# Eight lasting rooms for the expert weights, and the one-hot products of pair 14 moved ahead of pair 15's down projection

## The chip, the cores and the metric

The kernel runs on one core of a Trainium2 chip. TensorE (PE) multiplies, VectorE (DVE), ScalarE (ACT) and GpSimd (POOL) do the rest, and SP only issues transfers. SP, ACT and POOL each feed a queue of the same 16 DMA engines: in the profile q1 is SP's queue, q10 ACT's, q0 POOL's. The metric is the device time of one execution in microseconds (us), lower is better.

## The reference

Three transformer blocks follow one another on 512 tokens of width 1024, all in f32. The first holds windowed attention with a gated convolution, and then the mixture of experts that the change touches. The other two (attention and a squared-ReLU feed-forward each) come after it and are not touched. Cut to what matters, the mixture of experts is:

```python
h2 = rmsnorm(x, norm2_g)
g_logits = h2 @ w_rg + b_rg                # 4 groups
grp = argmax(g_logits)
e_in = (h2 @ w_re + b_re)[..., grp, :]     # the 8 experts of the group
top_p, top_i = top_k(softmax(e_in), 2)     # 2 experts for each token
gates = p_grp * top_p / sum(top_p)
...
hid = silu(xb @ w_gate[e]) * (xb @ w_up[e])     # 1024 -> 256, 32 experts
y   = hid @ w_down[e]                           # 256 -> 1024
x   = x + sum over a token's two experts of gate * y
```

The weights of the 32 experts are 100.7 MB, and every one is read once.

## The kernel before

**Pairs and pieces.** The experts are worked on two at a time: pairs 0 to 15, a pair on the two halves of TensorE. The weights of a pair come as three pieces of 2.10 MB, 128 partitions x 4096 f32: the two halves of gate and up (here gu p.0 and gu p.1) and the down projection (dn p). `moe_order` (L1605) gives the order of use: gu 0.0, gu 0.1, gu 1.0, gu 1.1, dn 0, gu 2.0, gu 2.1, dn 1 and so on to dn 14, dn 15. Places in this order are counted from 0.

**Rooms and rings.** A piece needs a room in SBUF. `c.rings` lists kinds of rooms, each with a function that makes the tiles, the number of rooms, and how many are taken: ring 0 the `raw` tiles that all other weights use (three of 1.05 MB), 1 two tiles `ew`, 2 the two slabs `esH`, `esL`, 3 the tile `ey` (tag `y0`), 4 four tiles `t`, and before the change 5 the tiles `we` (tags `wh` and `wl`, once each) and 6 the tiles `eq` (tag `yq`, once). A piece can lie in one room, or as two halves in rooms of two rings. `moe_jobs` (L1581) writes down for each piece which rings it takes; `Core._dma` (L89) issues the pieces strictly in the order of that list and stops at the first whose ring is not made yet or has no room; `_free` (L107) gives a room back when TensorE's use of the piece has been written into the program, and calls `_dma` again. In SP's queue the transfer itself then waits for the TensorE instructions that read the room last. A room of four 128x512 tiles is filled by four transfers with rows of 2 KB, a tile of 128x1024 by one with rows of 4 KB; the rows of the larger tiles are moved in pieces of 8 KB.

**Ahead of the routing.** While the attention's output projection still runs, five pieces are loaded (places 0, 4, 5, 6, 7 of the order). `moe` (L2015) then makes rings 3 and 6 and calls `_dma`: place 2 goes out in four transfers (`eq`). Place 1 is next in the list and takes ring 5, which is made only after `m.gates()`; so it, place 3 (ring 3) and place 8 are issued there, by ACT (`c._dma(queue=nc.scalar)`).

**The routing.** `Moe.norm` and `Moe.route` turn the tokens into rows and write them to DRAM: eight transfers of 0.26 MB with rows of 512 B (`hrows`, L1691, on ACT's queue), four of them in `route`. DVE works out the slots, and POOL gathers the token rows of a pair from `hrows` (`gather`, L1854) into `xg`; the gather waits for all eight writes. `turn` (L1894) turns them, and `gu` of pair 0 begins.

**The loop over pairs.** In turn p TensorE does gu of pair p, and then, for pair o = p - 1, the down projection. Up to pair 11 POOL scatters the result to DRAM (`yrows`, L1861). After the scatter of pair 11 `results` (L1870) reads them back, two of four blocks first (tiles `yr` and `y`, 512 rows of 2 or 4 KB altogether per block pair), and `add_results` turns and adds them. The last four pairs are added by one-hot products instead (`comb`, L1958): for each of eight blocks d of X, matmuls of y (two parts) with a one-hot matrix C, and an addition by DVE (L1960).

Before the change the products of pairs 12 and 13, four matmuls a block, are spread over turns 15 and 16; those of pairs 14 and 15, four a block, are done together in the last loop ("lastcomb"), between the first matmuls of the next block of the network:

```python
    for d in range(NB + 2):
        if d < NB:
            comb(NP - 2, d)
        if 1 <= d <= NB:
            nn[3](d - 1, X[:, d - 1])
```

Of the kernel before, what the change touches and what calls it, by code (L numbers as in the profile page):

```python
# [8 lines left out]
F32 = mybir.dt.float32  # L9
F32R = mybir.dt.float32r  # L10
# [7 lines left out]
D = 1024  # L18
NB = 8
EPS = 1e-6  # L20
NEG = -1e30
NRAW = 3
NSPL = 4
SPL = 512
# [14 lines left out]
class Core:  # L39


    def __init__(self, ctx, tc, aps):
        self.tc, self.nc, self.a = tc, tc.nc, aps
        self.ctx = ctx
        self.const = ctx.enter_context(tc.tile_pool(name="const", bufs=1))
        self.slab = ctx.enter_context(tc.tile_pool(name="slab", bufs=1))
        self.wp = ctx.enter_context(tc.tile_pool(name="wp", bufs=1))
        self.xs = ctx.enter_context(tc.tile_pool(name="xs", bufs=1, side="right"))
        self.wr = ctx.enter_context(tc.tile_pool(name="wr", bufs=1, side="right"))
        self.tmp = ctx.enter_context(tc.tile_pool(name="tmp", bufs=1, side="right"))  # L50
        self.ps = ctx.enter_context(tc.tile_pool(name="ps", bufs=1, space=bass.MemoryType.PSUM))
        self.dram = ctx.enter_context(tc.tile_pool(name="dr", bufs=1, space=bass.MemoryType.DRAM))
        self.jobs = []
        self.groups = []
        self.n_dma = 0
        raw = lambda: self.wr.tile([128, 2048], F32, name="raw", tag="raw", bufs=NRAW)
        self.rings = [[raw, NRAW, 0], None, None, None, None, None, None]
        self.n_split = 0
        self.cur = 0
        self.turns = 0  # L60
        self.now = 0
        self.blk_off = 0
        self.side = []
        self.due = []
        self.ratio = 1.0
        self.raw = {}
        self.spl = {}
        self.lows = []
        self.keep = {}
# [1504 lines left out]
NP = 16  # L1574
# [6 lines left out]
def moe_jobs(c):  # L1581

    gs = {}
    order = moe_order()

    def piece(i, *ring):
        n = order[i]
        w = c.a["e_w"][n // 3]
        o = 2 * (n % 3)
        if len(ring) == 1:  # L1590
            gs[n] = c.add_job(w[o:o + 2].rearrange("e p n -> p e n"), [(4096, 1)], split=False, ring=ring[0])
        else:
            gs[n] = sum((c.add_job(w[o + e], [(2048, 1)], split=False, ring=ring[e]) for e in range(2)), [])

    rooms = [(2,), (3,), (2,), (1,), (1,), (0, 0), (0, 4)]
    piece(0, 2)
    piece(4, 2)
    yield
    for i, ring in ((5, (1,)), (6, (1,)), (7, (0, 0)), (2, (6, 6)), (1, (5, 5)), (3, (3,)), (8, (0, 4))):
        piece(i, *ring)  # L1600
    for i in range(9, len(order)):
        ring = rooms.pop(0)
        if ring == (3,) and i > order.index(3 * NS + 3):
            ring = rooms.pop(0)
        rooms.append(ring)  # L1605
        piece(i, *ring)
    for n in order:
        c.groups += gs[n]
    yield
# [13 lines left out]
class Moe:  # L1623
# [327 lines left out]
    def comb(self, X, d, slots):  # L1951

        c, nc = self.c, self.c.nc
        acc = c.bank("S")
        n = 0
        for Y, C in slots:
            for y in Y:
                nc.tensor.matmul(acc, y[:, d * 128:d * 128 + 128], C, start=n == 0, stop=n == 2 * len(slots) - 1)  # L1958
                n += 1
        nc.vector.tensor_add(X[:, d], acc, X[:, d])  # L1960
# [47 lines left out]

        return self.pool2.tile([128, 4096], F32, name="ey", tag="y0")

    def quarters(self):
        return Row([self.pool2.tile([128, D], F32, name="eq", tag="yq", bufs=4) for _ in range(2)])


def moe(c, X, nn, next_g):  # L2015
    nc = c.nc
    c.mark("moe")
    m = c.moe
    m.pool2 = c.pool(m.es, "moe2")
    c.rings[3] = [m.early, 1, 0]  # L2020
    c.rings[6] = [m.quarters, 2, 0]
    c._dma()
    m.route(X)

    ohs = {}

    def onehot(p, n=2):
        ohs[p] = n, m.onehot(n, m.pos[:, :, 2 * p:2 * p + 2 * n])

    def slots(p):  # L2030
        n, oh = ohs[p]
        m.slots(n, oh, m.idc[:, p:p + n], m.idg[:, p:p + n], p < 2)

    def slots2(p):
        n, oh = ohs.pop(p)
        m.slots2(n, oh, m.info[:, :, p:p + n], m.gate[:, p:p + n], m.rs[:, p:p + n], m.idc[:, p:p + n], m.dest[:, p:p + n])

    gather = lambda p: m.gather(m.idg[:, p:p + 1], p)
    xg = {}
    for p in range(2):  # L2040
        onehot(p, 1)
        slots(p)
        xg[p] = gather(p)
    m.gates()
    c.rings[4] = [lambda: Row([c.t512() for _ in range(4)]), 1, 0]
    turns = iter(("wh", "wl"))

    def halves():
        tag = next(turns)
        return Row([c.wp.tile([128, SPL], F32, name="we", tag=tag, bufs=NSPL) for _ in range(4)])  # L2050

    c.rings[5] = [halves, 2, 0]
    c._dma(queue=nc.scalar)
    xt = {0: m.turn(xg.pop(0))}
    slots2(0)
    slots2(1)
    C = {}
    Y = {}
    held = []

    def w():

        release()
        j, r = c.take_raw()
        held.append(j)
        if len(c.jobs[j][0].shape) == 3:
            return [r[:, :2048], r[:, 2048:]]
        j, r2 = c.take_raw()
        held.append(j)
        return [r, r2]  # L2070

    def release():
        while held:
            c._free(held.pop(0))

    comb = lambda q, d: m.comb(X, d, [(Y[q], C[q]), (Y[q + 1], C[q + 1])])
    c.mark("experts")
    onehot(2)
    ht = {}
    for p in range(NP + 1):  # L2080
        if p < NP:
            hd = m.gu(xt.pop(p), w, m.rs[:, p:p + 1])
            release()
        if p == 0:
            slots(2)
            slots2(2)
        if p + 2 < NP:
            xg[p + 2] = gather(p + 2)
        if p + 1 < NP and p < 1:
            xt[p + 1] = m.turn(xg.pop(p + 1))  # L2090
        o = p - 1
        q = (o // 2 - 1) * 2
        ds = [] if q < NS else list(range(4)) if o % 2 == 0 else list(range(4, 8))
        for d in ds[:2]:
            comb(q, d)
        if o >= 0:
            tile = lambda dt: m.pool2.tile([128, D], dt, name="y", tag="yq", bufs=4)
            if o == NS:
                y = m.pool2.tile([128, 4, D], F32R, name="y4", tag="y0")
            if o < NS:  # L2100
                Y[o] = (tile(F32),)
            elif o < NP - 2:
                Y[o] = (y[:, 2 * (o - NS)], y[:, 2 * (o - NS) + 1])
            else:
                Y[o] = (tile(F32R), tile(F32R))
            m.down(ht.pop(o), w(), m.gate[:, o:o + 1], Y[o])
            release()
            if o < NS:
                m.scatter(o, Y[o][0])
            if o == NS - 1:  # L2110
                rooms = (lambda: Row([c.wp.tile([128, SPL], F32, name="yr", tag="wh", bufs=NSPL) for _ in range(4)]),
                         lambda: Row([tile(F32), tile(F32)]))
                res = [m.results(i, rooms[i]()) for i in range(2)]
            if o >= NP - 2:
                C[o] = m.spread(m.idc[:, o:o + 1], True)
        if 1 <= p < NP - 1:
            xt[p + 1] = m.turn(xg.pop(p + 1))
        for d in ds[2:]:
            comb(q, d)
        if p < NP:  # L2120
            ht[p] = m.turn_hid(hd)
        if o in (NS, NS + 1):
            b = 2 * (o - NS)
            for i in range(2):
                m.add_results(X, b + i, res[i])
            if o == NS:
                res = [m.results(2 + i, rooms[i]()) for i in range(2)]
            else:
                for q in (NS, NS + 1):
                    C[q] = m.spread(m.idc[:, q:q + 1], False)  # L2130
        if 1 <= p < 7:
            slots(2 * p + 2)
            slots2(2 * p + 2)
        if p < 6:
            onehot(2 * p + 4)
    m.beyond(X)
    c.mark("lastcomb")
    nn = c.norm_begin(next_g)
    accs = [c.bank(), c.bank()]
    c._split(c.cur + 1)  # L2140
    c._lows()
    for d in range(NB + 2):
        if d < NB:
            comb(NP - 2, d)
        if 1 <= d <= NB:
            nn[3](d - 1, X[:, d - 1])
            nc.sync.dma_start(c.xdr[:, d - 1], X[:, d - 1])
        if d >= 2:
            for acc in accs:
                for _ in c.block(1, *nn[:2], acc, first=d == 2, last=d == NB + 1, x0=d - 2):  # L2150
                    pass
    m.es.close()
    return nn[:3], accs
# [169 lines left out]
```

## Time and profile before

| | us |
|---|---|
| three runs, median (lowest to highest) | 1871.85 (1870.95 to 1873.17) |
| the profiled execution, its own time | 1871.83 |
| its span, first to last instruction | 1870.0 |
| expert stage: token rows complete, gather issued | 357.3 |
| first expert matmul | 364.9 |
| last loop begins, ends | 627.0, 648 |

All times below are us from the start of the span. The profiled execution agrees with the median; outside the span lie 1.8 us.

### The profile page before, as it was taken

How to read it: one execution, taken by the hardware profiler on the slowest of the kernel's cores; microseconds unless marked ns; L12 is line 12 of the kernel's file. 1: busy time of each engine (PE TensorE's matmuls, PEld its weight loads, DVE VectorE, ACT ScalarE, POOL GpSimd, SP SyncE). 2: the span in 40 equal slices, each digit the busy share in tenths (PEclk: the TensorE clock that was granted, in tenths of full speed). 3: DMA queues.
4: the chain of work that ended last, by engine and by line, in shares of the span. 5: the costliest groups of instructions: out<-in, count | busy, mean ns of one | idle time of the engine just before them, and what ended most of it. 6: DMA issues, size and time to landing. Idle time of an engine off the chain costs nothing.

```text
span 1870.0 us, 23372 instructions
## 1 busy us (share of the span) xinstructions
PE 1777.3 (95%) x8722; PEld 1326.1 (71%) x8722; DVE 1041.5 (56%) x1915; ACT 718.8 (38%) x1418; POOL 359.4 (19%) x392
## 2 busy tenths in 40 slices
PE   8999999799786999999999999999999999999998
PEld 6777787533233686667888888878777788888887
DVE  5765446543113767765655555564776565555555
ACT  6444334211000456664433333333666443333334
POOL 3212012111111251001211111121444221111111
PEclk9999999799997999999999999999999999999999
DMA  6124346599999320202322322243221322222321
GB/s 246 68 65 162 135 156 236 186 399 421 422 422 416 99 94 26 77 29 85 113 90 91 112 90 91 104 127 119 76 60 57 103 100 96 107 90 92 111 91 46
DMA packets 71831, 266.99 MB, mean 143 GB/s; under 512 B 24561, under 2 KB 31089, under 8 KB 46752
## 3 DMA queue, kind: packets, MB, share of 16 engines
q1 hardware_dynamic: 55120, 229.51, 33.2%
q0 software_dynamic: 9936, 27.47, 4.3%
q10 hardware_dynamic: 6656, 8.45, 1.3%
q8 instruction: 72, 1.18, 0.3%
q14 instruction: 47, 0.39, 0.1%
HBM read 251.57 MB, written 18.87 MB: 145 GB/s over the span
## 4 chain that ended last, share of the span: by engine, by line
PE 56%; DVE 6%; ACT 3%; issue 1%; DMA 0%; POOL 0%; POOLq 0%; DVEq 0%; ACTq 0%
PE psacc L227 15%; PE psacc L229 15%; PE psacc L228 15%; PE psT L709 2%; PE psO L861 2%; DVE wl L134 1%; PE psT L341 1%; PE psO L1440 1%; PE psS L1497 1%; PE psS L227 1%; PE psS L1185 1%; ACT wh L125 1%; PE psS L228 1%; PE psS L229 1%; ACT p L696 1%
## 5 line engine op out<-in xcount | busy, mean ns | idle before, releaser
L134 DVE TENSOR_TENSOR wl<-raw,wh 128x512 fp32r<-128x512 f32 x466 | 402.7, 867 | 246.3 <-ACT wh L125 244.8
L227 PE MATMUL psacc<-xh,wh 128*128 128x512 f32 x1008 | 407.4, 404 | 6.6 <-ACT wh L125 6.0
L125 ACT CAST wh<-raw 128x512 fp32r<-128x512 f32 x466 | 285.5, 617 | 321.6 <-PE psacc L228 272.4
L228 PE MATMUL psacc<-xl,wh 128*128 128x512 f32 x1008 | 394.6, 391 | 1.6 <-DVE xl L251 1.6
L229 PE MATMUL psacc<-xh,wl 128*128 128x512 f32 x1008 | 394.7, 392 | 0.1
L227 PEld LDWEIGHTS psacc<-xh,wh 128*128 128x128 f32 x1008 | 190.0, 189 | 56.0 <-issue 14.2
L229 PEld LDWEIGHTS psacc<-xh,wl 128*128 128x128 f32 x1008 | 189.8, 188 | 41.5 <-DVE wl L134 0.6
L228 PEld LDWEIGHTS psacc<-xl,wh 128*128 128x128 f32 x1008 | 190.3, 189 | 35.7 <-DVE xl L251 3.2
L227 PE MATMUL psacc<-uh,wh 128*128 128x512 f32 x480 | 187.0, 390 | 2.6 <-DVE x L453 2.6
L229 PE MATMUL psacc<-uh,wl 128*128 128x512 f32 x480 | 186.8, 389 | 0.0
L228 PE MATMUL psacc<-ul,wh 128*128 128x512 f32 x480 | 186.7, 389 | 0.0
L421 POOL TENSOR_TENSOR t<-t,rstd 128x512 f32<-128x512 f32 x64 | 82.9, 1295 | 526.6 <-ACT t L420 526.6
L453 DVE TENSOR_TENSOR x<-psacc,x 128x512 f32<-128x512 f32 x120 | 82.7, 689 | 125.4 <-PE psacc L229 125.4
L227 PEld LDWEIGHTS psacc<-uh,wh 128*128 128x128 f32 x480 | 90.1, 188 | 22.3 <-issue 3.8
L379 POOL TENSOR_TENSOR ss<-ss,t 128x512 f32<-128x512 f32 (+1 forms) x49 | 58.5, 1193 | 234.9 <-ACT t L372 234.6
L229 PEld LDWEIGHTS psacc<-uh,wl 128*128 128x128 f32 x480 | 90.1, 188 | 18.9
L228 PEld LDWEIGHTS psacc<-ul,wh 128*128 128x128 f32 x480 | 90.1, 188 | 18.5
L243 ACT CAST uh<-t 128x512 fp32r<-128x512 f32 x64 | 39.7, 621 | 131.3 <-DVE t L422 131.3
L709 PE MATMUL psT<-cst,p 128*128 128x128 f32 x448 | 77.1, 277 | 13.4 <-ACT p L696 12.6
L709 PEld LDWEIGHTS psT<-cst,p 128*128 128x128 f32 x448 | 55.2, 140 | 42.6 <-ACT p L696 22.6
L420 ACT ACTIVATE t<-psacc 128x512 f32<-128x512 f32 x64 | 38.3, 599 | 80.8 <-PE psacc L229 80.8
L1914 DVE SCALAR_TENSOR_TENSOR hd<-psS,rs,sl 128x256 f32<-128x256 f32 x16 | 7.7, 484 | 107.9 <-ACT sl L1913 107.9
(493 smaller groups left out, 2707.7 us busy)
## 6 DMA issues: line engine op xcount, KB each, us to landing
raw<-ffn SPq DMA_DIRECT2D x64, 1024.0 KB
ew<-e_w SPq DMA_DIRECT2D x14, 2048.0 KB
raw<-e_w SPq DMA_DIRECT2D x17, 1024.0 KB
esH<-e_w SPq DMA_DIRECT2D x7, 2048.0 KB
esL<-e_w SPq DMA_DIRECT2D x7, 2048.0 KB
ey<-e_w SPq DMA_DIRECT2D x5, 2048.0 KB
raw<-w_in_a SPq DMA_DIRECT2D x8, 1024.0 KB
raw<-od_qk SPq DMA_DIRECT2D x8, 1024.0 KB
```

The source lines that it names most:

```text
L125: nc.scalar.copy(h[:, :n], r)
L134: self.nc.vector.tensor_sub(l, r, h)
L227: nc.tensor.matmul(acc, wh, xh, start=first, stop=False)
L228: nc.tensor.matmul(acc, wh, xl, start=False, stop=False)
L229: nc.tensor.matmul(acc, wl, xh, start=False, stop=last)
L243: nc.scalar.copy(h, src)
L379: self.nc.gpsimd.tensor_add(s, s, q)
L420: nc.scalar.activation(r, acc, AF.Relu)
L421: nc.gpsimd.tensor_mul(r2, r, st["r2"])
L453: nc.vector.tensor_add(X[:, d], acc, X[:, d])
L709: nc.tensor.transpose(t[:, o:o + 128], p[:, m * 128:m * 128 + 128], c.ident)
L861: self.c.nc.tensor.matmul(o[64 * hh:64 * hh + 64], self.V[:, kb, v:v + 64], pt[hh][:, kb], start=kb == 0, stop=kb == 3, skip_group_check=True)
```

## The change

- The one-time rooms are laid out as follows: ring 5 four tiles `wl`, ring 8 a half `yq` (place 1 of the order takes 8 and 5, once); ring 7 four tiles `wh`, ring 6 a half `yw`. Rooms (7, 6) become a lasting room, used in rotation up to place 30 (gu 10.1).
- The rotation has eight rooms and not seven: (2,), (2,), (1,), (1,), (0, 0), (7, 6), (3,), (0, 4). A piece takes the room of the piece eight places before it (seven before the change), the tenth piece that of the first.
- Five pieces are loaded during the output projection as before, now places 0, 2, 3, 4, 5. All rings but 4 are made at the start of `moe`, so places 1, 6, 7 and the first half of 8 go out there on SP: 14 transfers, 7.34 MB, where four transfers of 2.10 MB went out. ACT issues only the second half of place 8 after the gates.
- The results y of pairs 0 to 11 rotate over two tiles `yq` and not four; pair 14 and 15's, and the second room of `results`, take `yq` and `yw`.
- The one-hot products of pairs 12 and 13 are all done in turn 15; those of pair 14 alone, two matmuls for each of eight blocks, in turn 16 ahead of pair 15's down projection; the last loop does pair 15 alone, two matmuls a block.

```diff
-    rooms = [(2,), (3,), (2,), (1,), (1,), (0, 0), (0, 4)]
+    rooms = [(2,), (2,), (1,), (1,), (0, 0), (7, 6), (3,), (0, 4)]
+    last = {(7, 6): order.index(3 * NS - 1), (3,): order.index(3 * NS + 4)}
     piece(0, 2)
-    piece(4, 2)
+    piece(2, 2)
     yield
-    for i, ring in ((5, (1,)), (6, (1,)), (7, (0, 0)), (2, (6, 6)), (1, (5, 5)), (3, (3,)), (8, (0, 4))):
+    for i, ring in ((3, (1,)), (4, (1,)), (5, (0, 0)), (1, (8, 5)), (6, (7, 6)), (7, (3,)), (8, (0, 4))):
         piece(i, *ring)
     for i in range(9, len(order)):
-        ring = rooms.pop(0)
-        if ring == (3,) and i > order.index(3 * NS + 3):
-            ring = rooms.pop(0)
-        rooms.append(ring)
-        piece(i, *ring)
+        while i > last.get(rooms[0], i):
+            rooms.pop(0)
+        rooms.append(rooms.pop(0))
+        piece(i, *rooms[-1])
...
-    def quarters(self):
-        return Row([self.pool2.tile([128, D], F32, name="eq", tag="yq", bufs=4) for _ in range(2)])
+    def half(self, tag):
+
+        return Row([self.pool2.tile([128, D], F32, name="eh", tag=tag, bufs=2) for _ in range(2)])
...
+    quarters = lambda tag: Row([c.wp.tile([128, SPL], F32, name="we", tag=tag, bufs=NSPL) for _ in range(4)])
     c.rings[3] = [m.early, 1, 0]
-    c.rings[6] = [m.quarters, 2, 0]
+    c.rings[5] = [lambda: quarters("wl"), 1, 0]
+    c.rings[6] = [lambda: m.half("yw"), 1, 0]
+    c.rings[7] = [lambda: quarters("wh"), 1, 0]
+    c.rings[8] = [lambda: m.half("yq"), 1, 0]
     c._dma()
     m.route(X)
...
-    c.rings[5] = [halves, 2, 0]
     c._dma(queue=nc.scalar)
...
-    comb = lambda q, d: m.comb(X, d, [(Y[q], C[q]), (Y[q + 1], C[q + 1])])
+    comb = lambda qs, d: m.comb(X, d, [(Y[q], C[q]) for q in qs])
...
-        q = (o // 2 - 1) * 2
-        ds = [] if q < NS else list(range(4)) if o % 2 == 0 else list(range(4, 8))
-        for d in ds[:2]:
-            comb(q, d)
+        qs = {NP - 2: (NS, NS + 1), NP - 1: (NP - 2,)}.get(o)
+        ds = [] if qs is None else list(range(NB))
+        for d in ds[:4 if o == NP - 2 else NB]:
+            comb(qs, d)
...
-        for d in ds[2:]:
-            comb(q, d)
+        for d in ds[4:] if o == NP - 2 else []:
+            comb(qs, d)
...
         if d < NB:
-            comb(NP - 2, d)
+            comb((NP - 1,), d)
```

## Rows read from the trace of the kernel before

**Rows 1.** The page, slices of 46.75 us: DMA share in tenths, and GB/s.

```profile
DMA  6124346599999320202322322243221322222321
GB/s 246 68 65 162 135 156 236 186 399 421 422 422 416 99 94 26 77 29 85 113 90 91 112 90 91 104 127 119 76 60 57 103 100 96 107 90 92 111 91 46
```

**Rows 2.** Windows of the expert stage: length, busy us by engine, PE clock, DMA share, GB/s.

```profile
343.00:352.00 9.00, 7.61 (x40) 5.61 (x38) 5.95 (x26) 3.42 (x6) 0.00 (x0) 0.64 0.77 263
352.00:356.00 4.00, 1.08 (x20) 0.59 (x18) 2.73 (x12) 0.96 (x3) 0.00 (x0) 0.93 0.72 199
356.00:361.00 5.00, 0.27 (x4) 0.18 (x4) 4.00 (x23) 0.20 (x1) 3.04 (x4) 0.50 0.32 93
...
388.00:470.00 82.00, 78.00 (x462) 31.55 (x462) 30.68 (x86) 9.58 (x19) 13.16 (x13) 1.00 1.02 420
470.00:553.00 83.00, 64.94 (x287) 23.29 (x284) 11.72 (x20) 7.30 (x14) 9.11 (x9) 0.94 1.02 421
```

**Rows 3.** Timeline of POOL: start, length, instruction, idle time before it and its releaser.

```profile
357.29 1.10 POOL L1854 DMA_INDIRECT xg<-hrows,idg  x1 [16.88 <-DVE oh L1814]
...
389.81 1.01 POOL L1861 DMA_INDIRECT yrows<-y,dest  x1 [10.99 <-DVE xt L1896]
...
468.71 1.01 POOL L1861 DMA_INDIRECT yrows<-y,dest  x1 [10.85 <-DVE xt L1896]
...
553.01 1.00 POOL L1861 DMA_INDIRECT yrows<-y,dest  x1 [16.80 <-DVE xt L1896]
```

**Rows 4.** Timeline of SP's queue: when the transfers are issued.

```profile
343.14 1.75 SPq L101 DMA_DIRECT2D eq<-e_w  x4
...
384.82 0.38 SPq L104 DMA_DIRECT2D ey<-e_w  x1
```

**Rows 5.** Timeline of PE, the beginning of the expert stage.

```profile
361.99 1.94 PE L1894 MATMUL psT<-cst,xg 128*128 128x128 f32 x8 [4.61 <-DMA xg<-hrows,idg]
...
364.89 5.84 PE L1908 MATMUL psS<-esH,xt 128*64 128x512 f32 x16
...
381.18 3.60 PE L1908 MATMUL psS<-ey,xt 128*64 128x512 f32 x16
```

**Rows 6.** DMA from 322.0 to 326.4: queue, packets, MB, share; and the issues.

```profile
q1 hardware_dynamic: 115, 0.94, 72.3%
...
hrows<-t ACTq DMA_DIRECT2D x1, 256.0 KB
```

**Rows 7.** DMA from 326.4 to 329.0.

```profile
q10 hardware_dynamic: 528, 0.26, 33.6%
```

**Rows 8.** DMA from 350.5 to 355.5.

```profile
q10 hardware_dynamic: 2112, 1.05, 75.5%
```

**Rows 9.** DMA from 584 to 592.

```profile
q1 hardware_dynamic: 299, 2.30, 68.2%
q0 software_dynamic: 299, 1.08, 33.1%
```

**Rows 10.** DMA from 570 to 574.

```profile
q0 software_dynamic: 253, 0.89, 54.9%
q1 hardware_dynamic: 247, 0.77, 47.4%
```

**Rows 11.** Timeline of PE, the end of the expert stage.

```profile
579.64 1.94 PE L1884 MATMUL psT<-cst,y 128*128 128x128 f32 x8 [4.31 <-DVE y L1879]
...
610.14 2.12 PE L1958 MATMUL psS<-C,y 128*128 128x512 f32 x8
...
623.48 2.10 PE L1958 MATMUL psS<-C,y 128*128 128x512 f32 x8
627.00 3.03 PE L1958 MATMUL psS<-t,y 128*128 128x512 f32 x12 [1.42 <-DVEq L1968]
```

**Rows 12.** Window of the last loop, columns as in rows 2.

```profile
628.30:648.10 19.80, 18.18 (x75) 13.48 (x74) 19.42 (x22) 12.35 (x22) 10.89 (x8) 1.00 0.49 160
```

**Rows 13.** DVE's additions of the one-hot products: busy us, mean ns, idle before.

```profile
L1960 DVE TENSOR_TENSOR x<-psS,x 128x512 f32<-128x512 f32 x16 | 10.8, 684 | 0.8 <-PE psS L1958 0.5
```

More of the change, by code (lines that the diff above doesn't have):

```diff
@@ L56, in __init__ @@
         raw = lambda: self.wr.tile([128, 2048], F32, name="raw", tag="raw", bufs=NRAW)
-        self.rings = [[raw, NRAW, 0], None, None, None, None, None, None]
+        self.rings = [[raw, NRAW, 0], None, None, None, None, None, None, None, None]
         self.n_split = 0
@@ L2045, in moe @@
     c.rings[4] = [lambda: Row([c.t512() for _ in range(4)]), 1, 0]
[L2046 to L2050, printed above, removed]
-    c.rings[5] = [halves, 2, 0]
     c._dma(queue=nc.scalar)
@@ L2091, in moe @@
         o = p - 1
-        q = (o // 2 - 1) * 2
-        ds = [] if q < NS else list(range(4)) if o % 2 == 0 else list(range(4, 8))
-        for d in ds[:2]:
-            comb(q, d)
+        qs = {NP - 2: (NS, NS + 1), NP - 1: (NP - 2,)}.get(o)
+        ds = [] if qs is None else list(range(NB))
+        for d in ds[:4 if o == NP - 2 else NB]:
+            comb(qs, d)
         if o >= 0:
-            tile = lambda dt: m.pool2.tile([128, D], dt, name="y", tag="yq", bufs=4)
+            tile = lambda dt, tag: m.pool2.tile([128, D], dt, name="y", tag=tag, bufs=2)
             if o == NS:
@@ L2100, in moe @@
             if o < NS:
-                Y[o] = (tile(F32),)
+                Y[o] = (tile(F32, "yq"),)
             elif o < NP - 2:
@@ L2104, in moe @@
             else:
-                Y[o] = (tile(F32R), tile(F32R))
+                Y[o] = tuple(tile(F32R, ("yq", "yw")[o % 2]) for _ in range(2))
             m.down(ht.pop(o), w(), m.gate[:, o:o + 1], Y[o])
@@ L2111, in moe @@
                 rooms = (lambda: Row([c.wp.tile([128, SPL], F32, name="yr", tag="wh", bufs=NSPL) for _ in range(4)]),
-                         lambda: Row([tile(F32), tile(F32)]))
+                         lambda: m.half("yw"))
                 res = [m.results(i, rooms[i]()) for i in range(2)]
```

## The prediction

> **What bounds the kernel now.** I read the page's slices first: the DMA engines are full in five of forty slices, from about 370 to 600 us, at some 420 GB/s, and nowhere else for that long [rows 1]. That is the expert stage, the only part the change touches. The windows then show what precedes it: from 343 to 361 the engines are partly idle (263, 199 and 93 GB/s), from 388 on they run at 420 without a gap [rows 2].
>
> Inside the full stretch the limit changes over. The scatter of pair p comes 13.15 us after that of pair p - 1 as long as TensorE never waits: (468.71 - 389.81) / 6 for pairs 0 to 6 [rows 3]. At that pace pair 11 would be scattered at 389.81 + 11 x 13.15 = 534.5; it is scattered at 553.01. So 18.5 us are lost between pairs 7 and 11, where PE's busy time falls from 78.0 us in 82 to 64.9 in 83 while the DMA stays full [rows 2]. From pair 7 the stream of weights sets the pace, and the scatter of pair 11, after which the results are read back, is as late as the stream is.
>
> Behind it the limit changes twice more. PE stands until the results are there (4.31 us before 579.64), and from 610.14 it has work up to the 1.42 us ahead of the last loop at 627.00 [rows 11]. In that loop DVE is busy 19.42 of 19.80 us [rows 12].
>
> **The change part by part.**
>
> *The early issue.* Four transfers of 2.10 MB go out at 343.14 [rows 4]. Now it is 14 of 7.34 MB, from the same place in SP's queue and released by the same end of the projection, so again at 343.1. Today 2.37 MB pass by 352 (9 us x 263 GB/s) [rows 2], 2.10 of them these weights; the first 2.1 MB of the new load will take as long, to about 350.5. The other 5.24 MB need 12.5 us at 420 GB/s: 363.
>
> ACT writes the last four blocks of token rows from 350 on. Alone they are 1.05 MB in 2112 packets and take 75.5% of the engines' time in 5.0 us, 3.8 us of work [rows 8]. What becomes of such a write beside weights shows earlier: one of 0.26 MB was issued together with a weight load of 1 MB, and until 326.4 all 115 packets were the load's [rows 6]; the write's packets came after 326.4 [rows 7]. Where two queues did share, they took turns packet by packet: 299 and 299 in 8 us [rows 9]. Of the weights some 1150 packets are left at 350.5 (512 of 2 KB, 256 of 4, 384 of 8), fewer than the rows' 2112, so either way the rows end last: both loads together at 363 + 3.8 = 366.8. I take 366. The gather, issued at 357.29 today [rows 3], needs all the rows, so it goes out near 366.3, and the first turn (361.99) and pair 0 (364.89) [rows 5] follow: TensorE starts its experts 9 us late. Bounds: under 1 us if the writes are served as they arrive, 10.5 if they are issued a little later too.
>
> [...]
>
> *The eighth room.* The last dip of the stream ends with the issue at 384.82, place 10 of the order, which waits for gu 1.1 (381.18 + 3.60 = 384.8) [rows 4, 5]. With eight rooms place 10 takes the room of place 2, gu 1.0, which is free when gu 1.1 begins, at 381.18 today. So relative to TensorE the stream becomes continuous 3.6 us earlier, and the later places get their rooms in time (one each 13.15 / 3 = 4.4 us, a piece takes 5.0). But TensorE is 9 us late: all that was issued early has landed by about 370, and SP has nothing to issue until pair 0 gives a room back. The bytes gained in 352 to 363 are lost again there. Stream: 9 - 3.6 = +5.4 us (bounds -3 and +7). TensorE's own 9 us don't show: pair 11 without waits would be scattered at 543.5, with the later stream it is at 558.4. So that scatter moves by +5.4.
>
> *The results.* After it 512 packets of results and 128 of a gather come in before TensorE can go on, in turns with the weights: POOL got 253 packets in 4 us while most of the weights' were of 2 KB [rows 10], 299 in 8 against 8 KB [rows 9]. Today the piece with 2 KB rows in flight there is dn 13 (rooms 0 and 4); by the new rotation that room holds gu 15.1, two pieces later, and dn 13 lies in `ew`. At 37 packets a us the 640 take 17 us, at 63 a us 10; today has both kinds, so half the difference, 3.5, is the most that can be lost. +2 us (bounds 0 and +3.5).
>
> *The moved products.* 16 matmuls leave the last loop and stand ahead of pair 15's down. PE does eight in 2.1 us there [rows 11], so 16 take 4.2; the eight more additions of 0.684 us [rows 13] reach into the down, which hides them. The eight matmuls that lay behind the down (623.48 [rows 11]) are gone, and the 1.42 us behind them overlap less: another 0.8. The last loop gives little back, since DVE's work in it is unchanged (eight additions, eight splits, the low parts of the weights) and fills 98% of it [rows 12]; I give it 1.0. Sum +4 us. Bounds: 0.8 if the loop shortens by all 4.2, +5 if not at all.
>
> ACT issues four and not fourteen transfers after the gates, and waits for them beside PE's first pair [rows 5]: 0. The two tiles `yq` return after two pairs, 26 us: 0. The next block's first loads now wait for gu 15's rooms and not for those of pair 14's gate and pair 13's down; they have the 17 us from 610.14 to 627 to land [rows 11]: 0, and about 7 us on the last loop, a load's way, if that cover were gone.
>
> **Sum.** +5.4 + 2 + 4 = +11.4 on 1871.83 (the span of 1870.0 and 1.8 outside it; the median of the runs is the same within 0.1): 1883.2.
>
> **The rivals.**
>
> *Rows served at once, the rest paid.* If ACT's writes pass the queued loads, the start moves 0.6 us, the stream -3, and with +2 and +4 the sum is +3: 1875. For it: rows 9, where one queue doesn't wait for another's backlog. Against it: rows 6 and 7.
>
> *The change does what it says, and the kernel is faster.* Place: the gather at 357.29. From 343 to 361 the engines have 9.4 us idle (3.4 + 2.1 + 3.9 by rows 2). If the two extra pieces, 4.2 MB or 10 us of stream, go there and stay ahead to the end, 10 of the 18.5 us that pairs 7 to 11 lose are saved; with the 4 of the products -6: 1866. It decides where the start moves by less than 4 us and the stream doesn't pause while pair 0 runs. Against it: the rooms are full by 370 and come back at TensorE's pace.
>
> *The queues take turns by whole transfers.* Each of the four writes (1 us) then waits for one of SP's (0.6 or 1.2 us, 5 for a 2.1 MB one, at 420 GB/s). The rows land near 361, the start moves 4 us, the stream +0.5, and the sum is +6.5: 1878. [...]
>
> *Rows last, products free.* The last loop shortens by all 4.2: +8, 1880.
>
> **How the numbers follow.** Rows last 0.47 (own range 1877 to 1888), turns 0.12, products free 0.05: slower, 0.64. Rows served at once 0.18, within 0.2% (3.7 us, about what a measurement of this kernel can tell from no change). The change as it says 0.18 (1862 to 1870): faster. The range from 1868 to 1888 holds nearly all of the first four and the near edge of the last, some 0.8.
>
> **What would show it.** The last `hrows` packets near 366 and the first gather behind them; gu of pair 0 near 374; a hole in the DMA row between 370 and 382, and then 420 GB/s; the scatter of pair 11 near 558.4; the last loop beginning some 11 us after 627 and no more than 1 us shorter. I am wrong if the gather still goes out before 359, if the last loop takes under 18 us, or if PE waits for weights elsewhere than in pairs 7 to 12.

## The result, and the profile after

The changed kernel takes 1888.95 us (median of four runs, 1887.45 to 1889.36) beside 1871.4 for the kernel before on the same chip: slower, ratio 1.0091, 95% interval 1.0073 to 1.0108. I had forecast 1883.2 and, as the top of the range, 1888. The sign and the places of the loss are those of the prediction; three of its sizes are not, and one price was missing altogether. The term that missed by most is that of the moved products: +4 forecast, 7.6 measured at the end of the last loop. The profiled execution after took 1889.34, with a span of 1887.6.

| us from the start of the span | before | after | later by |
|---|---|---|---|
| first gather issued | 357.29 | 361.39 | 4.1 |
| gu of pair 0 | 364.89 | 374.27 | 9.4 |
| scatter of pair 11 | 553.01 | 556.52 | 3.5 |
| last results turned | 579.64 | 586.67 | 7.0 |
| gu of pair 15 done | 610.14 | 617.63 | 7.5 |
| last loop begins | 627.00 | 642.20 | 15.2 |
| last loop's matmuls over (L301) | 648.43 | 663.52 | 15.1 |
| span | 1870.0 | 1887.6 | 17.6 |

The windows of the stage (columns as in [rows 2]) show the bargain that was struck at its beginning: 297 and 267 GB/s where 199 and 93 stood, then 170 where 412 had stood, 284 where 216, and 400 where 420. The first two lines are those of the kernel before that [rows 2] leaves out, the others are after the change.

```profile
374.00:384.00 10.00, 8.48 (x58) 3.71 (x58) 4.15 (x13) 0.85 (x2) 2.06 (x2) 1.00 1.01 412
384.00:388.00 4.00, 4.00 (x20) 1.15 (x16) 0.48 (x1) 1.16 (x2) 0.00 (x0) 1.00 0.73 216
```

```profile
343.00:352.00 9.00, 7.57 (x40) 5.52 (x39) 5.49 (x24) 2.99 (x5) 0.00 (x0) 0.68 0.79 262
352.00:356.00 4.00, 1.34 (x18) 0.84 (x16) 3.01 (x13) 1.17 (x2) 0.00 (x0) 0.86 0.93 297
356.00:361.00 5.00, 0.52 (x8) 0.35 (x8) 3.68 (x23) 0.42 (x2) 0.00 (x0) 0.55 0.85 267
...
374.00:384.00 10.00, 9.21 (x53) 3.24 (x53) 3.55 (x17) 1.76 (x2) 0.00 (x0) 0.85 0.48 170
384.00:388.00 4.00, 3.17 (x20) 1.56 (x22) 3.45 (x11) 0.37 (x1) 2.05 (x2) 1.00 0.75 284
388.00:470.00 82.00, 78.43 (x462) 31.04 (x460) 28.79 (x83) 9.20 (x18) 12.13 (x12) 1.00 0.98 400
```

SP's queue, for [rows 4], says why the rows were not last. The issues of the second `eh` pair stretch over 6.7 us: one leaves at 352.64, the other at 359.0, and `ey` and `raw` (3.15 MB) only behind it. By the landing times in the trace the second left when the `hrows` write eight transfers before it on the two queues had landed (358.94). The two tell of their landing by the same semaphore, and so it is with six of SP's issues here: each leaves 0.02 to 0.07 us after the last transfer of its semaphore has landed.

```profile
343.66 0.80 SPq L101 DMA_DIRECT2D eh<-e_w  x2
344.56 7.40 SPq L101 DMA_DIRECT2D we<-e_w  x8
352.64 6.69 SPq L101 DMA_DIRECT2D eh<-e_w  x2
359.38 0.43 SPq L104 DMA_DIRECT2D ey<-e_w  x1
...
389.91 0.38 SPq L104 DMA_DIRECT2D esL<-e_w  x1
```

POOL's timeline, for [rows 3], and PE's, for [rows 5]. From the gather's issue to TensorE it is now 9.98 us and not 4.70.

```profile
361.39 1.10 POOL L1854 DMA_INDIRECT xg<-hrows,idg  x1 [20.46 <-DVE rcol L1801]
...
556.52 0.99 POOL L1861 DMA_INDIRECT yrows<-y,dest  x1 [14.16 <-DMA t<-e_w]
```

```profile
371.37 1.94 PE L1894 MATMUL psT<-cst,xg 128*128 128x128 f32 x8 [13.47 <-DMA xg<-hrows,idg]
...
374.27 4.98 PE L1908 MATMUL psS<-esH,xt 128*64 128x512 f32 x16
```

The 5.3 us more are made of two parts. The first is a wait before any of the gather's packets (POOL's queue, q0) passes: in the trace they begin 4.3 us after its issue and not 1.8. From 361.4 to 365.6 there is none after the change (first fence); before it, from 359.0 to 361.4, they have the engines almost to themselves (second fence). Why they begin later, no run tests.

```profile
q1 hardware_dynamic: 240, 1.36, 78.8%
q10 hardware_dynamic: 134, 0.24, 19.0%
```

```profile
q0 software_dynamic: 141, 0.52, 72.9%
q10 hardware_dynamic: 30, 0.06, 8.8%
```

The second part is what they then meet. The DMA from 365 to 371: three queues with 190, 160 and 194 packets, so each has about every third turn, and SP's packets are the largest (1.47 MB of 2.43). Equal counts alone would also fit turns of several rows; but of the packets that begin 3 or 4 ns before the end of another, one of q1 stands behind one of q0 164 times, q10 behind q1 177 and q0 behind q10 166 times, and all other orders together make 73.

```profile
q1 hardware_dynamic: 190, 1.47, 58.2%
q0 software_dynamic: 160, 0.59, 24.8%
q10 hardware_dynamic: 194, 0.36, 17.5%
```

PE at the end of the stage, for [rows 11]: the results are waited for 7.11 us, and between pair 15's down (its second half ends 635.29 + 1.89) and the last loop 5.03 us pass. The first matmuls of the loop take 0.49 us each (2.93 / 6), those of before 0.25 (3.03 / 12).

```profile
586.67 1.94 PE L1884 MATMUL psT<-cst,eh 128*128 128x128 f32 x8 [7.11 <-DVE eh L1879]
...
617.63 3.92 PE L1958 MATMUL psS<-C,y 128*128 128x512 f32 x16
...
628.98 4.62 PE L1958 MATMUL psS<-t,y 128*128 128x512 f32 x16
...
635.29 1.89 PE L1934 MATMUL psO<-esL,ht 128*64 128x512 f32 x8
642.20 2.93 PE L1958 MATMUL psS<-t,y 128*128 128x512 f32 x6 [5.03 <-DVEq L1968]
```

Three windows around it (columns as in [rows 2]): TensorE idle for 5 us, then 5 us at a granted clock of 0.56. The last one, which begins inside that stretch, is the loop as in [rows 12]: DVE is still its limit, 19.31 of 19.80 us.

```profile
637.20:642.20 5.00, 0.00 (x0) 0.00 (x0) 1.31 (x3) 1.82 (x3) 0.00 (x0) 0.76 0.02 7
642.20:647.20 5.00, 5.00 (x11) 3.30 (x12) 4.55 (x8) 2.96 (x6) 0.51 (x1) 0.56 0.31 110
...
643.40:663.20 19.80, 16.80 (x62) 11.70 (x61) 19.31 (x21) 12.34 (x22) 10.83 (x8) 0.92 0.49 159
```

The wait is named after L1968, the branch in `beyond`, which jumps over further rounds for experts with more than 64 tokens. DVE's two instructions of that line (duration ns min/median/max, first and last start): it branches at 638.6 and goes on at 641.8. Before, these stood at 626.3 and 626.8.

```profile
L1968 DVEq COMPARE_BRANCH  x1: 72/72/72, 638.6 to 638.6; - x1
L1968 DVEq EVENT_SEMAPHORE  x1: 21/21/21, 641.8 to 641.8; - x1
```

### The profile page after: what moved, and what is told of

Same layout as the page of the kernel before. It is cut to its first block, busy times and chain, and to the rows that moved or that the text cites. A ratio compares the mean times of both kernels' runs of the same rounds, so it can differ in the third digit from the quotient of the medians.

```text
span 1887.6 us, 23435 instructions
## 1 busy us (share of the span) xinstructions
PE 1780.7 (94%) x8722; PEld 1328.0 (70%) x8722; DVE 1047.0 (55%) x1923; ACT 718.5 (38%) x1418; POOL 358.9 (19%) x392
## 4 chain that ended last, share of the span: by engine, by line
PE 56%; DVE 6%; ACT 3%; issue 1%; DMA 0%; POOL 0%; POOLq 0%; DVEq 0%; ACTq 0%
PE psacc L227 15%; PE psacc L229 15%; PE psacc L228 14%; PE psT L709 2%; PE psO L861 1%; DVE wl L134 1%; PE psT L341 1%; PE psO L1440 1%; PE psS L227 1%; PE psS L1497 1%; PE psS L1185 1%; PE psS L228 1%; PE psS L229 1%; ACT wh L125 1%; ACT p L696 1%
```

## The experiments

My theory after reading: the early issue makes TensorE start 9.4 us late, of which the eighth room gives some back (+3.5 at the scatter of pair 11); results beside 8 KB packets cost 3.5; the moved products cost 7.7, part of it at the branch. The main rival: the products are nearly free, and the rooms do it all. Each ratio below is to the kernel before, run beside it on the same chip (medians 1871.3 to 1872.9).

**The rooms alone.** The changed kernel with the products as before.

```diff
-    comb = lambda qs, d: m.comb(X, d, [(Y[q], C[q]) for q in qs])
+    comb = lambda q, d: m.comb(X, d, [(Y[q], C[q]), (Y[q + 1], C[q + 1])])
...
-            comb((NP - 1,), d)
+            comb(NP - 2, d)
```

> The changed kernel with the one-hot products put back where they were: only the rooms and the early issue are new. My theory (start late by 9, eighth room gives part back, results 3.5 dearer; products 7.7, of which about 5 are matmuls and end of the down and 2.8 a branch that nothing covers): the scatter of pair 11 stays at 556.5, the last loop begins near 634.5, and the time is 1889 - 7.7 = 1881. Rival, products cost only the 4 of my prediction and the rest of the loss is the rooms': 1885. Rival, the products cost nothing: 1889.

**The products alone.** The kernel before with the reverse of that diff.

> The kernel before with only the products moved. My theory: nothing changes up to the end of gu 15 (610.1), the last loop begins 7.7 later (634.7), DVE stands some 3 us at the branch ahead of it, the loop is as long as before, and the time is 1871.4 + 7.7 = 1879. By my prediction's term (+4): 1875.5. Rival, products free: 1871.5.

Measured: 1880.79 (ratio 1.0044, 1.003 to 1.0058) and 1880.42 (1.0043, 1.0029 to 1.0057). That is 8.6 and 8.3 us above the kernel before beside them, 16.9 of the 17.5 of the whole change: the two halves add up, and the products are not free. PE of the products alone: the down ends at 629.29, 5.7 later than before (621.66 + 1.89), and 4.42 us are lost behind it.

```profile
627.40 1.89 PE L1934 MATMUL psO<-ew,ht 128*64 128x512 f32 x8
633.71 2.90 PE L1958 MATMUL psS<-t,y 128*128 128x512 f32 x6 [4.42 <-issue]
```

**Eight rooms, early issue held back.** Place 1 alone goes out at 343, as many bytes as before; the other rings are made after the gates. Products as before. Against the changed kernel, without the products:

```diff
-    c.rings[3] = [m.early, 1, 0]
     c.rings[5] = [lambda: quarters("wl"), 1, 0]
-    c.rings[6] = [lambda: m.half("yw"), 1, 0]
-    c.rings[7] = [lambda: quarters("wh"), 1, 0]
     c.rings[8] = [lambda: m.half("yq"), 1, 0]
     c._dma()
...
     m.gates()
+    c.rings[3] = [m.early, 1, 0]
+    c.rings[6] = [lambda: m.half("yw"), 1, 0]
+    c.rings[7] = [lambda: quarters("wh"), 1, 0]
```

> The eight rooms of the changed kernel, but only place 1 (2.10 MB in six transfers) goes out at 343; the rest is issued by ACT after the gates, as before; products as before. My theory: the gather goes out within 1 us of 357.3 and TensorE starts within 1 us of 364.9; the eighth room then makes the stream 3.6 earlier, the scatter of pair 11 comes near 549.5; the results cost up to 3.5 more, so the last loop begins at 624 to 627 and the time is 1868 to 1872. Rival, the loss lies in the rooms and their rotation and not in the early issue: scatter of pair 11 at 556, 1880.

Measured: 1874.05 (1.0008, 0.9999 to 1.0017): 6.7 below the rooms alone, but above the 1868 to 1872 expected. The gather leaves at 356.89 and the scatter of pair 11 comes 5.1 us before that of [rows 3], more than the 3.6 expected. But the last results are turned at 578.67, only 1.0 earlier: TensorE waits 7.21 us for them and not the 4.31 of [rows 11]. So in this trace the results eat what the stream had gained. How much that is, the scatter tells only roughly: in the six traces with seven rooms (before, products alone, 20 idle instructions, small rows, and the two without the branch), which hardly differ in what runs ahead of it, it comes 184.7 to 188.6 us after gu of pair 0 begins, in the nine with eight rooms 182.1 to 184.9. The gap that the room closes shows in the window from 384 to 388 (below): 437 GB/s where 216 stood, 0.9 MB or some 2 us of stream. The last loop begins 1.7 earlier than before (625.33), and yet the time is no better; what is lost behind it is taken up under the sum.

```profile
356.89 1.10 POOL L1854 DMA_INDIRECT xg<-hrows,idg  x1 [16.52 <-DVE oh L1814]
...
547.88 0.99 POOL L1861 DMA_INDIRECT yrows<-y,dest  x1 [14.26 <-DMA t<-e_w]
```

```profile
384.00:388.00 4.00, 3.89 (x22) 1.58 (x18) 1.56 (x3) 0.69 (x1) 0.00 (x0) 1.00 1.04 437
```

```profile
578.67 1.94 PE L1884 MATMUL psT<-cst,eh 128*128 128x128 f32 x8 [7.21 <-DVE eh L1879]
```

**`ey` held back.** The changed kernel, `c.rings[3] = [m.early, 1, 0]` moved behind the gates; with `ey` (place 7) the whole of place 8, which follows it in the list, is issued there.

> The changed kernel, but place 7 (ring 3, the tile ey) and what follows it in the list are issued by ACT after the gates; places 1 and 6 (4.19 MB in 12 transfers) still go out early on SP. My theory, the late start has two parts: the rows' writes are held up by the early weights (the gather goes out 4.1 late, and still does), and the gather then shares the engines with two other queues and not one (10.0 us from its issue to TensorE and not 4.7): with ey behind ACT it shares with one, and TensorE starts 4 to 5 late, not 9.4. That is some 4.5 earlier than in the changed kernel, the stream and the scatter of pair 11 follow, 1884.5. Rival, the start is all one delay of the rows: 1889. Rival, the stream is bound by its bytes and doesn't follow TensorE's start: scatter of pair 11 still at 556, 1889.

Measured: 1888.66 (1.0093, 1.0077 to 1.0108), no difference. The expectation missed: with `ey` in ACT's queue (issued at 358.16) the gather still takes 8.74 us (360.91 to 369.65; 9.98 in the changed kernel). In the build held back it takes 4.6 (356.89 to 361.49). TensorE starts 1.7 earlier, not 4.5, the scatter of pair 11 comes at 554.63 (1.9 earlier), and 1.4 of it are left at the last results. The delay ahead of the gather's first packet, which neither this theory nor a rival had, is about half of what the gather lost in the changed kernel (4.3 us for 1.8, of 9.98 for 4.70).

**Small rows beside the results.** On the build with the early issue held, places 42 to 45 in transfers of 512 columns; then the same on the changed kernel and on the kernel before, and once without place 42.

```diff
+                if self.n_dma in self.small:
+                    for k in range(0, int(np.prod(ap.shape[1:])), 512):
+                        s = ap if len(ap.shape) == 2 else ap[:, k // 2048]
+                        queue.dma_start(o[:, k:k + 512], s[:, k % 2048:k % 2048 + 512])
```

> The kernel with eight rooms and only place 1 issued early, and in addition places 42 to 45 of the order (the weights in flight while the results of pairs 0 to 11 are read back) are loaded in transfers of 512 columns: rows of 2 KB where they were of 8. My theory, packets of both queues take turns one by one, so the 640 packets of results and gather then pass at some 60 a us and not 38 (10.7 us and not 17): TensorE waits about 1 and not 7.2 us ahead of the last results, the last loop begins some 6 earlier, 1874 - 6 = 1868, faster than the kernel before. Rival, the engines are full and the bytes decide: no change, 1874. Rival, the weights that are now later hold up pairs 14 and 15: 1871 to 1874, with the wait moved to their matmuls.

> The changed kernel, unaltered but for the same small rows at places 42 to 45. My theory, its results are dear because weights of 8 KB rows are in flight beside them: the 7.1 us ahead of the last results fall to about 1.4, the last results begin near 581 and not 586.7, the time is 1889 - 5 = 1884. Rival, they are dear because more is queued (the stream is further ahead): the wait stays, 1889.

> The kernel before, seven rooms and all, with places 42 to 45 of the order loaded in transfers of 512 columns (rows of 2 KB). It asks what the eighth room is worth beside the faster results. If the room's 5 us at the scatter of pair 11 carry through: the scatter stays at 553, the results come 4 to 5 earlier, but pairs 13 to 15 then wait for weights, 1869 to 1870, that is 2 to 3 above the build with eight rooms and small rows (1867.1). Rival, the rows' size is the whole gain and the room brings nothing: 1867.

> The build with eight rooms, the early issue held and small rows, but place 42 in rows of 8 KB again. If place 42, whose 16 small transfers are still being issued when the results come, costs the pairs behind more than it gives: 1 to 2 below 1867.1. If the results meet place 42: the wait ahead of them is back by 2 to 4 us, 1869 to 1871.

Measured: held and small 1867.13 (0.9976, 0.9967 to 0.9985), **faster than the kernel before**; the changed kernel with small rows 1883.59 (1.0058), 5.4 less than the changed kernel, as expected (its last results are turned at 579.88, its last loop begins at 636.63, 5.6 earlier); the kernel before with small rows 1871.58 (0.9997, 0.9988 to 1.0006), no change; without place 42 1869.66 (0.9984, 0.9975 to 0.9993), with a wait of 3.75 us ahead of the results: they do meet place 42. The DMA from 564 to 572, the held build first and then with small rows: both times the two queues have about the same number of packets, but some 305 a side in one and some 640 in the other, and what POOL moved is 1.06 and 1.98 MB.

```profile
q1 hardware_dynamic: 305, 2.34, 69.3%
q0 software_dynamic: 307, 1.06, 32.6%
```

```profile
q0 software_dynamic: 631, 1.98, 61.5%
q1 hardware_dynamic: 661, 1.25, 40.6%
```

The wait ahead of the last results falls from 7.21 to 1.43 us (line numbers of this build are 10 higher):

```profile
573.57 1.87 PE L1894 MATMUL psT<-cst,eh 128*128 128x128 f32 x8 [1.43 <-issue]
...
585.70 1.08 PE L1944 MATMUL psacc<-ew,ht 128*64 128x512 f32 x4 [1.56 <-DMA ew<-e_w]
```

The second row is the bill: the weights that stood back are now late for a down, and of the 5.1 us won at the last results 1.3 are left at the last loop (624.07 and 625.33). Nearly all of the rest goes in that down, which takes 8.4 us and not 3.6 (1.78 us of waits, and a granted clock of 0.83 from 574 to 600). The stream is slower too: 404 GB/s from 564 to 572, where the held build moves 426, and 338 from 574 to 600. By the medians the time falls by 6.9, between the two profiled executions only by 2.0: this one took 1870.90, 3.8 above its build's median. That the build is faster is thus measured; the path by which its other runs gain the rest is not shown.

In the kernel before the same rows bring the last loop forward by 2.4 (624.60), which its time doesn't show. What the eighth room is worth by itself is thus not settled to better than some 4 us: 0.5 by the last loops of the two traces, 4.5 by the medians, which are from two chips (3.9 by the ratios).

**The wait at the branch.** First try: two of pair 14's eight blocks behind the down, so that DVE has additions queued when it reaches the branch, as before the change.

```diff
-        for d in ds[:4 if o == NP - 2 else NB]:
+        for d in ds[:4 if o == NP - 2 else 6]:
...
-        for d in ds[4:] if o == NP - 2 else []:
+        for d in ds[4:] if o == NP - 2 else ds[6:]:
```

> The changed kernel, but of pair 14's eight blocks of products two (four matmuls, two additions) stand behind pair 15's down. My theory, DVE's branch starts earlier under the two additions: the 5.03 us ahead of the last loop fall to 1.5 to 2.5, the loop begins about 2.6 earlier, 1886.4. Rival, the wait at the branch is there wherever the additions stand: 5 us stay, 1889.

Measured: 1887.03 (1.0081), near the 1886.4 expected, but not for the reason expected. The theory fell: DVE goes on 3.1 us after the branch with two additions in front of it, 3.2 without, and 5.27 us pass from the down's end to the loop (635.77 to 641.04), of which 1.2 are now matmuls.

In the changed kernel, this build and the products alone DVE lost 2.9 to 3.2 us here (in the last one only after one instruction behind the jump), in the kernel before, the rooms alone and the held build 0.5 to 0.6. The moved products put eight more additions ahead of the branch, so I asked whether the place of the branch in the code mattered. Two builds test that with instructions that only clear an idle column:

```diff
+        if p in (2, 3, 4, 5, 6, 7, 8, 9):
+            for _ in range(12):
+                nc.vector.memset(idle, 0.0)
```

> The changed kernel with 96 instructions of DVE added that clear one idle column, twelve in each of turns 2 to 9, where DVE is idle two thirds of the time. My first theory (the branch is dear because no additions stand in front of it) fell with the run that put two behind the down. New theory: the 3.1 us are the fetch of the code behind the branch's jump; where the target lies in the 8 KB of code fetched ahead, the jump takes 0.5 us (the kernel before, and the two builds with the products put back), where it lies behind them the code is fetched only after the jump (the three builds with the products moved). 96 more instructions move branch and target into the next 8 KB: the jump takes 0.5 us again, 2.5 less on the path, 1886.5. Rival, the wait belongs to the moved products whatever the code's place: 1889.

> The kernel before with 20 such idle instructions of DVE, five in each of turns 3 to 6, and nothing else. By the theory of the code's place the branch then stands where it stands in the changed kernel: DVE resumes some 3.1 us after it and not 0.5, the last loop begins 2.5 later, 1874.3. Rival, the place is of no matter: 1871.8.

Measured: 1887.59 (1.0079) and 1878.46 (1.0037, 1.0023 to 1.005). DVE's rows of L1968, the changed kernel with 96 idle instructions and the kernel before with 20:

```profile
L1968 DVEq COMPARE_BRANCH  x1: 72/72/72, 639.4 to 639.4; - x1
L1968 DVEq EVENT_SEMAPHORE  x1: 21/21/21, 640.0 to 640.0; - x1
```

```profile
L1968 DVEq COMPARE_BRANCH  x1: 72/72/72, 626.7 to 626.7; - x1
L1968 DVEq EVENT_SEMAPHORE  x1: 21/21/21, 629.6 to 629.6; - x1
```

DVE's wait goes both times as the theory of the code's place says: it is taken away by instructions that do nothing, and put into the kernel before by others. That it is a fetch of code is less sure. The 8 KB of the theory are the size of the packets of instructions in the traces (51 of 8 KB on q14 in the kernel before); that so much lies fetched ahead of a jump is my assumption, and no run shows it. In the second build one 8 KB packet of instructions is fetched at 627.8, inside the wait; in the kernel before none is between branch and going on; but in the first build too one follows the branch, at 639.6, and DVE goes on at 640.0. And the times are off on both sides. In the first, TensorE still stands 4.11 us ahead of the loop (5.03 in the changed kernel): its semaphore comes at 640.0, its first matmul at 642.09, with no wait that the trace explains. A fetch of 16 KB of instructions ends 1.3 us before that, so I take it that TensorE's own code came late too, hidden behind DVE's in the changed kernel; that is argued, and no run tests it. The last loop begins at 642.09, 0.1 us earlier than in the changed kernel, so nothing is won there, and the time of 1887.59 lies between the expected 1886.5 and the rival's 1889. In the second, the loss is 7 and not 2.5: the loop begins 2.8 later (629.79), and after the stand of 3.76 us the clock is down in its first 5 us (0.71 in this window, 1.00 before), so the loop takes 22.6 and not 21.4 us. That makes 4.0; another 2.7 of the span are lost behind the loop (see the sum).

```profile
629.80:634.80 5.00, 4.72 (x14) 3.52 (x15) 3.54 (x6) 2.08 (x4) 0.00 (x0) 0.71 0.17 59
```

**The products without the branch.** What they cost by themselves: the products alone, and the kernel before, each without the call of `beyond` (the rounds that these inputs don't need are left out).

```diff
-    m.beyond(X)
```

> The kernel before with only the products moved, and without the branch ahead of the last loop: the call of beyond is left out, which holds the further rounds for an expert with more than 64 tokens and is jumped over with these inputs. My theory, of the 8.3 that moving the products cost with the branch, the jump is 2.5 to 3 and the slower clock after the 4.4 us stand another 1.3: without it TensorE stands about 2 us after the last down (DVE's and ACT's way for y alone), the clock stays up, the last loop is 1 to 1.5 shorter than the 21.4 of before, and the time is 3.5 to 4.5 above the same kernel with the products where they were (the run beside it). Rival, the stand has nothing to do with the branch: the 4.4 us stay, and the difference is 7 to 8.

> The kernel before without the branch, the base for the run beside it (the same call left out). There the jump took 0.5 us, between two queued additions and the last loop: 0.5 to 1 less than before, 1871. If the branch costs more than its own 0.5 even there (the engines meeting at it): 2 or more less, 1869 or below.

Measured: 1878.17 (1.0032, 1.002 to 1.0044) and 1871.57 (0.9996, 0.9987 to 1.0005). The products cost 6.6 without the branch, more than the 3.5 to 4.5 I expected: by the times the branch makes 1.7 of the 8.3, not 4, and the intervals are wider than that; the traces below carry it better. PE at the last loop of both: 2.06 us of stand, which is y's way through ACT and DVE, against none.

```profile
630.82 1.39 PE L1958 MATMUL psS<-t,y 128*128 128x512 f32 x3 [2.06 <-DVE t L1948]
```

```profile
627.00 2.96 PE L1958 MATMUL psS<-t,y 128*128 128x512 f32 x12
```

From gu 15's end it is 21.64 us to the loop against 15.25 (+6.4), and the loop takes 21.0 against 22.4 (-1.4): +5.0. With the branch the same two legs give 23.94 - 16.86 = +7.1 and 0.0. The -1.4 is against a loop that is itself 1.0 longer than that of the kernel before (21.4). And the clock did not stay up, as I had expected it to without the branch: after the stand of 2.06 us the granted clock is 0.66 in the first 5 us of the loop.

```profile
630.80:635.80 5.00, 4.98 (x14) 3.33 (x15) 4.69 (x8) 3.25 (x6) 0.79 (x1) 0.66 0.28 105
```

## Why the prediction was wrong, point by point

The start and the room came out near the forecast, the start by two errors that cancel. What failed is the term of the moved products (+4 forecast, 7.6 measured), which took the stand behind the last down for 0.8 us and the branch in it for a fixed price; and 2.5 us behind the last loop stood in no term.

**The early issue: total right by luck, its way wrong.** TensorE's start moves 9.4 us (I said 9). The step that failed is "either way the rows end last". It rests on [rows 6] and [rows 7] showing a whole load pass ahead of a write. From 326.4 to 329.0 SP's queue moved this too, a line that [rows 7] leaves out, so nine tenths of that load went first and the rest shared with the write:

```profile
q1 hardware_dynamic: 29, 0.11, 10.1%
```

The step took all 7.34 MB as queued ahead of the rows; 3.15 MB of it left SP only at 359.4, and the rows, beside the rest (766 packets of their queue and 440 of SP's from 352 to 356), were down by 360.5 and not 366. I then gave the gather its old 4.7 us, and it took 10. Two errors of 5 us cancel: the rows were as the rival of whole transfers had them (gather 4 later), the rest, a gather that begins late and then takes turns with two queues, I had not priced at all. That rival's turns by whole transfers were my assumption, and no run shows them: the three queues show 190, 160 and 194 packets that alternate one by one. The price is tested: holding the issue back gives 6.7 us.

**The eighth room: mechanism right, its size not settled.** I counted 3.6 us. Against the one trace of [rows 3] it is 4.7 to 5.9 at the scatter of pair 11 (-5.1 + 0.4 in the held build; 3.5 - 9.4 in the changed one), but in the other traces with seven rooms that scatter comes up to 3.4 us earlier after gu of pair 0, so 1.3 would fit as well. Place 10 goes out 15.6 us after pair 0's start (389.91 - 374.27) where it was 19.9. In this trace the scatter is 3.5 late and not 5.4.

**The results: the upper bound.** I took +2, about the middle of 0 to 3.5; what is in flight there now is all in rows of 8 KB. 305 packets in 8 us are 38 a us, the rate of that bound (37), and the loss is 7.0 - 3.5 = 3.5. Small rows take 5.4 off the changed kernel. All traces bear it out: from the scatter of pair 11 to the last results it is 26.5 to 28.8 us with seven rooms, 29.8 to 30.8 with eight, and 23.2 to 23.5 where places 42 to 45 have small rows.

**The moved products: the term that failed.** I had 4.2 + 0.8 - 1.0 = 4, at most 5; alone they cost 8.3 and in the changed kernel 7.6 by the end of the loop. Without the branch they are +6.4 and -1.4. The 16 matmuls take 4.62 and not 4.2; beside them DVE adds without a pause. Behind the down it is 1.8 and not 0.8: I had counted what overlapped less with the 1.42 us of the branch, not y's way of 2.06 us that the eight matmuls had covered in full. The last loop gives back 1.4 without the branch, nothing in the changed kernel: the stand before it has grown to 5 us, the granted clock of its first 5 us is 0.56, and the loop is as long as before. But the clock falls behind the 2.06 us stand too (0.66), so it is a price of the uncovered stand, and the branch only adds to it.

**The branch: not in the prediction.** [Rows 11] named it in the wait of 1.42 us ("DVEq L1968"), and I read that as a fixed price. It is not: about 2 us of the loss (8.3 - 6.6 by the times, 7.1 - 5.0 by the traces) go with the branch, by the times not clear of the noise: with it the stand is 4.4 us long and not 2.1. That the time goes into code fetched behind the jump is argued, from two builds in which idle instructions move DVE's wait; no run shows the fetch as the cause.

**Sum.** At the end of the loop +3.5, +3.5, +0.5 to gu 15's end, and +7.6 for products and branch: 15.1, of which I had 11.4. The other 2.5 come later: 1.2 in one stretch near 1484, where the clock of the profiled execution falls (0.94 from 1460 to 1490, 1.00 before), the rest in small steps. Eleven of the fourteen profiled builds with any edit show that dip, three and the kernel before don't; why it comes, is open. With the dip the span behind the start of L301's matmuls is 1223.6 to 1224.7 us, in the three without it 1222.4 to 1222.5, in the kernel before 1221.6. The runs of the kernel before themselves go from 1870.0 us at a mean granted clock of 0.986 to 1874.7 at 0.980, so a part of the 2.5 may belong to the execution and not to the change.

What I said would show it: gu of pair 0 near 374 (374.27), the hole after 370, the scatter near 558 (556.5), the loop beginning later and not over 1 us shorter, and PE waiting for weights only in pairs 7 to 12 held. The rows near 366 did not (360.5), nor 420 GB/s after the hole (400 up to 470), nor the loop some 11 us later (15.2).

## What to carry to other kernels

Bytes moved earlier were no gain here, where a write and a gather had to pass them (6.7 us by the rooms alone and the held build): price every small transfer that shares the engines with the new ones, the gather behind as well as the write, by the number of queues and the size of their packets. Where a critical read runs beside a bulk load, cut the bulk load into small rows for just that stretch: here that turned an even result (1.0008) into a gain of 0.24% by the times, though the stream was slower with the small rows (404 GB/s for 426) and a later piece came late. Work moved ahead of a last step uncovered the latency behind that step (a stand of 2.06 us without the branch, against none); what covered it before is to be priced at its full length, the idle engine's clock included (0.66 behind that stand).

## What the runs showed of the hardware

- Queues with rows of 2, 4 and 8 KB took turns packet by packet: 305 to 307, 661 to 631, and 190 to 160 to 194 with three. Rows of 512 B beside rows of 2 KB did not pass in equal numbers (766 to 440 packets from 352 to 356 after the change), and nine tenths of a load of 1 MB passed before a write that was issued 0.5 us after it [rows 6, 7].
- A gather of 128 rows of 4 KB had its first packet 1.8 us after its issue in the kernel before, where the engines were idle (DMA share 0.00 in those 1.8 us), and 4.3 us after it in the changed kernel, where they were full (0.98).
- The price of the same jump changed with instructions far ahead of it: DVE goes on 0.5 us after the branch in the kernel before and 2.9 with 20 instructions ahead that do nothing, 3.2 in the changed kernel and 0.6 with 96 of them. The branch instruction itself takes 72 ns in all four.
- TensorE's clock after a stand: in the 5 us behind a stand of 2.06, 3.76 and 5.03 us the granted clock was 0.66, 0.71 and 0.56 (2.93 us for six matmuls behind the last), behind one of 1.42 us it was 1.00 (12 in 3.03).
